# A q/kv group turned token-major: 512 + 192 columns, ScalarE sums of squares, and latents turned back by transposes

## The chip, the cores and the metric

The kernel runs on one core of one Trainium2 chip. The metric is the device time of one execution in microseconds (us). TensorE multiplies matrices: it loads a stationary operand of up to 128 x 128 and streams the columns of a moving operand past it. VectorE, ScalarE and GpSimd do the elementwise work, SyncE issues most of the DMAs.

## The reference

Two layers of a streaming encoder over 256 positions of width 2048. The part that the change touches is the latent attention's input: of the projection `h @ w_in`, 704 columns are the query latent (384), the key/value latent (256) and a rotary key (64).

```
proj = h @ w_in[l]
uv, q_c, kv_c, k_r, sb, sc, sh, ag = jnp.split(proj, IN_SPLITS, axis=-1)
def rms_norm(x, gain, eps=RMS_EPS):
    y = xf * lax.rsqrt(jnp.mean(jnp.square(xf), axis=-1, keepdims=True) + eps)
    return y * gain
...
q = rms_norm(q_c, q_norm_g) @ w_uq            # 4 heads of 128 + 64 (rotary)
kv = rms_norm(kv_c, kv_norm_g) @ w_ukv        # 4 heads of 128 + 128
k_rope = apply_rope(k_r, cos, sin)
... scores, block-causal mask, softmax, times v
```

Beside this stand a gated MLP (columns u, v), a short convolution (sb, sc, sh), and a convolution of 31 taps (ag), then an output projection and a feed-forward block. All of it is float32.

## The kernel before

The projection is computed in groups of columns, in the order D (the ag columns), U and V, B (the q/kv columns), C (sc and sh), E (sb). A group runs over 16 k-tiles of 128 rows of `w_in`, two or four of them a unit. `run` calls `stream` for each unit: it loads the unit's weights (`weights`), issues the products of the unit before, advances the modulation stream (`pump`: a DMA of `w_mod` and a `macc` step on VectorE, L235), and takes `bg` pieces of background work. When a group's last products have been issued, its `then` function follows: for group B that is `mix_b`, the whole attention, followed in program text by group C's products.

In the first layer group B's weights are plain float32 tiles (`wexact`), multiplied by the normalised input `hF`. In the second layer each weight tile is split in two parts of type fp32r: ScalarE makes `whi` (L455), VectorE makes `wlo` (L456), and three products are taken, whi with hT's high and low part, wlo with the high part.

Group B before is channel-major: a 128 x 128 block of weights is stationary, 256 tokens stream past, and six blocks of 128 channels (768 columns, the last 64 of them unused) fill three PSUM banks of 2 x 256. `mix_b` then squares five blocks on ScalarE (`sqB`), sums the squares over partitions with ten matmuls against ones (`ps_ss`), makes rr on VectorE, raises it to -0.5 on GpSimd (`power`, L105), spreads the kv part over partitions by a diagonal matrix and a matmul (`dgB`, `ps_rkv`), and multiplies kvr by it. The q norm is applied later, in the softmax scale. `qg`, `kvr` and `kc` feed the matmuls `ps_qn`, `ps_kn`, `ps_v` and `ps_kr`.

Background work in both layers is, above all, the 31-tap convolution of group D: `tap(j, k)` is one instruction on VectorE over 128 channels (convD, L834; in the changed file L868), 120 of them a layer. In the text they are queued a few per unit (`STEPS`: B takes 7 a unit in the first layer, 5 in the second). The instructions' final order on each engine is not that of the text: a scheduler in the framework lists them by readiness when the program is built, and each engine's list is then fixed.

PSUM has six banks for group sums (`accp`) and two for the rest (`msp`); weight splits have four buffers each of whi and wlo.

Of the kernel before, what the change touches and what calls it, by code (L numbers as in the profile page):

```python
# [39 lines left out]
STEPS = [  # L40
    dict(B=7, C=8, up=2),
    dict(U=6, B=5, C=6, E=6, up=2),
]
# [7 lines left out]
def encoder_kernel(ctx: ExitStack, tc: tile.TileContext, A: dict, consts: bass.AP, out: bass.AP):  # L51
    nc = tc.nc
    pe, act, dve, pool = nc.tensor, nc.scalar, nc.vector, nc.gpsimd
# [7 lines left out]
    smallp = ctx.enter_context(tc.tile_pool(name="smallp", bufs=2))  # L61
# [7 lines left out]
    def tmp_tile(name):  # L69
        return tmpp.tile([P, 512], F32, tag="tmp", name=name)  # L70

    def ms_tile(name):
        return msp.tile([P, 512], F32, tag="ms", name=name)

    def acc_tile(name):
        return accp.tile([P, 512], F32, tag="acc", name=name)

    def mm(o, lhsT, rhs, start, stop):
        pe.matmul(o, lhsT, rhs, start=start, stop=stop, skip_group_check=True)  # L79
# [4 lines left out]
    def slot(name, dtype=F32):  # L84
        return slotp.tile([P, 1024], dtype, tag="slot", name=name)
# [4 lines left out]
    ident = cst[:, 0:128]  # L90
# [3 lines left out]
    cosT = cst[:, 512:768]  # L94
    sinT = cst[:, 768:1024]
# [3 lines left out]
    ones = ones_r.bitcast(F32)  # L99
# [367 lines left out]
    hT = []  # L467
# [9 lines left out]
    def group(w, c0, width, name, then, ntm=0, nk=2, hF=None, bg=0, spare=0):  # L477

        ncm = (width - 512 * ntm) // P
        box = {}

        def products(item, u):
            if u == 0:
                box["c"] = [acc_tile(f"{name}_c{i}") for i in range((ncm + 1) // 2)]
                box["t"] = [[acc_tile(f"{name}_t{t}{i}") for i in range(ntm)] for t in range(2)]
                box["h"] = list(hT)
            for part in (range(0, min(4, ncm)), range(4, ncm)):
                for k, (hi, lo) in enumerate(item):  # L490
# [36 lines left out]

    def group2(w, c0, name, then, bg=0, spare=0):
# [21 lines left out]

        return KT // nk, load, products, lambda: then(box["c"]), bg

    hN, first = [], []

    def first_group(w, c0, then):
# [251 lines left out]
    def mixers(l, w_in, Y, hF=None, between=None):  # L807
        pm = PM[l]
        CW = lambda k, j: pm[:, k * 4 + j : k * 4 + j + 1]
        QG = lambda j: pm[:, 124 + j : 125 + j]  # L810
        KVG = lambda j: pm[:, 127 + j : 128 + j]
# [135 lines left out]
                )  # L947


        def mix_b(cps, _):  # L950
# [9 lines left out]
            qg = slot("qg")[:, :768].rearrange("p (j s) -> p j s", j=3)  # L960
            kvr = slot("kvr")[:, :768].rearrange("p (j s) -> p j s", j=3)
            bank = [(cps[i // 2], (i % 2) * S) for i in range(6)]
            sq = [tmp_tile("sqB0"), tmp_tile("sqB1"), tmp_tile("sqB2")]
            sqs = []
            for i in range(5):
                ps, o = bank[i]
                s = sq[i // 2][:, (i % 2) * S : (i % 2) * S + S]
                act.activation(out=s, in_=ps[:, o : o + S], func=AF.Square)
                sqs.append(s)
            for j in range(3):  # L970
                ps, o = bank[j]
                act.activation(out=qg[:, j, :], in_=ps[:, o : o + S], func=AF.Copy, scale=QG(j))
            for j in range(2):
                ps, o = bank[3 + j]
                dve.tensor_scalar(out=kvr[:, j, :], in0=ps[:, o : o + S], scalar1=KVG(j), scalar2=None, op0=ALU.mult)
            ps, o = bank[5]
            kc, ks = tmp_tile("kc"), None
            dve.tensor_tensor(out=kc[0:64, 0:S], in0=ps[0:64, o : o + S], in1=cosT[0:64, :], op=ALU.mult)
            dve.tensor_tensor(out=kc[0:64, S : 2 * S], in0=ps[0:64, o : o + S], in1=sinT[0:64, :], op=ALU.mult)
            ps = ms_tile("ps_ss")  # L980
# [6 lines left out]
            dve.tensor_scalar(  # L987
                out=rr[:, 0:2], in0=ps[:, 0:2], scalar1=1.0 / Q_LORA, scalar2=RMS_EPS, op0=ALU.mult, op1=ALU.add
            )
            dve.tensor_scalar(  # L990
                out=rr[:, 2:4], in0=ps[:, 2:4], scalar1=1.0 / KV_LORA, scalar2=RMS_EPS, op0=ALU.mult, op1=ALU.add
            )
            power(rr[:, 4:8], rr[:, 0:4])
            dve.tensor_scalar(out=rr[:, 4:6], in0=rr[:, 4:6], scalar1=ATT_SCALE, scalar2=None, op0=ALU.mult)
            dg = tmp_tile("dgB")
            for t in range(2):
                dve.tensor_scalar(
                    out=dg[:, t * P : (t + 1) * P], in0=ident, scalar1=rr[:, 6 + t : 7 + t], scalar2=None, op0=ALU.mult
                )
            ps = ms_tile("ps_rkv")  # L1000
            mm(ps[:, :S], ones, dg[:, :S], True, True)
            for j in range(2):
                dve.tensor_tensor(out=kvr[:, j, :], in0=kvr[:, j, :], in1=ps[:, :S], op=ALU.mult)

            rope = slot("rope").rearrange("p (j s) -> p j s", j=4)
            ps = ms_tile("ps_kr")
# [167 lines left out]
    def by_pieces(l, w_in, hF, between, mix_d, mix_u, gelu_v, mix_v, mix_b, mix_c, mix_e):  # L1174
# [50 lines left out]
        for q, (k0, nkt) in enumerate(PIECES):  # L1225
# [42 lines left out]
            gelu_v(t, sums["V"][t])  # L1268
        mix_v()
        phase(l, "B")  # L1270
        run(group(w_in, C_Q, 768, f"B{l}", mix_b, hF=hf, bg=STEPS[l]["B"]))
        phase(l, "C")

        def mix_ce(cps, tps):
# [260 lines left out]
```

## Time and profile before

| | us |
|---|---|
| median of three runs | 2290.1 |
| lowest and highest | 2289.65, 2292.27 |
| profiled execution | 2285.5 |
| its span | 2283.7 |

In the profile's rows PE is TensorE's matmuls and PEld its weight loads, DVE is VectorE, ACT is ScalarE, POOL is GpSimd, SPq the queue from which SyncE issues DMAs. A row of the timeline gives the start and the length in us of a merged run of equal instructions, its line, what it writes and reads, and how many there are (xN); in brackets, how long the engine had idled before it and what ended that. Matmuls overlap, so what one costs in a stream is read from the distance of two starts, not from its length. A plain float32 matmul shows as two records, an fp32r one as one. A row of the waits gives total us, times, longest. L79 is the helper that issues nearly all matmuls, so its rows are told apart by tile names.

### The profile page before, as it was taken

What the parts mean: (1) busy time and instruction counts of PE and PEld (TensorE: products, weight loads), DVE (VectorE), ACT (ScalarE), POOL (GpSimd) and SP (SyncE); (2) the same over time, 40 slices, a digit from 0 to 9 for tenths busy, and PEclk for the clock granted to TensorE, in tenths of its full rate; (3) what the DMA queues carried; (4) which work ended last, traced back from release to release, by engine and by line L of the source; (5) the groups of instructions that cost most, each with busy time, mean ns of one, the idle gap of its engine ahead of it and who ended that gap; (6) DMA issues with size and microseconds to landing.
All of it is one profiled execution on the core that took longest, in us unless ns stands there. A gap on an engine that the chain in (4) does not pass through costs nothing. (4 is left out here: it accounts for less than half of the span.)

```text
span 2283.7 us, 30024 instructions
## 1 busy us (share of the span) xinstructions
PE 2226.7 (98%) x11682; PEld 1859.8 (81%) x11682; DVE 1788.8 (78%) x2270; ACT 1049.8 (46%) x1525; POOL 35.3 (2%) x59
## 2 busy tenths in 40 slices
PE   5899999999999999999999999999999999999998
PEld 4688886478888888887887999877888888888886
DVE  6878998598888898998976799787776565665676
ACT  2221141355554544544556434556555554454553
POOL 2000000000000000000000000000000000000000
PEclk9999999999999999999999999999999999999999
DMA  9999889778998988888974666876765556555554
GB/s 348 368 335 342 304 301 393 301 267 304 319 329 302 323 312 327 317 316 304 319 258 148 200 214 240 291 268 223 247 223 190 184 182 199 186 196 190 193 194 147
DMA packets 224566, 605.21 MB, mean 265 GB/s; under 512 B 14548, under 2 KB 27076, under 8 KB 202660
## 3 DMA queue, kind: packets, MB, share of 16 engines
q1 hardware_dynamic: 223576, 602.30, 74.7%
q8 instruction: 91, 1.49, 0.3%
q0 software_dynamic: 848, 1.01, 0.1%
q14 instruction: 51, 0.42, 0.0%
HBM read 601.16 MB, written 2.10 MB: 264 GB/s over the span
## 5 line engine op out<-in xcount | busy, mean ns | idle before, releaser
L456 DVE TENSOR_TENSOR wlo<-wraw,whi 128x1024 fp32r<-128x1024 f32 (+1 forms) x624 | 749.6, 1214 | 315.5 <-ACT whi L455 309.4
L455 ACT CAST whi<-wraw 128x1024 fp32r<-128x1024 f32 (+1 forms) x624 | 649.2, 1047 | 727.2 <-PE g_c L79 204.4
L79 PE MATMUL v_c<-hT,whi 128*128 128x512 f32 x1408 | 493.1, 394 | 0.0
L79 PE MATMUL g_c<-hT,whi 128*128 128x512 f32 x1280 | 448.2, 394 | 0.0
L79 PE MATMUL v_c<-hT,wlo 128*128 128x256 f32 x1408 | 394.3, 280 | 0.0
L79 PE MATMUL d<-whi,a 128*128 128x512 f32 x1344 | 387.9, 390 | 0.0
L235 DVE SCALAR_TENSOR_TENSOR macc<-wmod,cact,macc 128x2048 f32<-128x2048 f32 x150 | 351.6, 2344 | 17.1 <-DMA wmod<-in_w_mod_dram 16.8
L79 PE MATMUL g_c<-hT,wlo 128*128 128x256 f32 x1280 | 358.4, 280 | 0.0
L79 PEld LDWEIGHTS v_c<-hT,whi 128*128 128x128 f32 x1408 | 263.9, 187 | 61.0
L79 PEld LDWEIGHTS d<-whi,a 128*128 128x128 f32 x1344 | 252.9, 188 | 52.4
L79 PEld LDWEIGHTS g_c<-hT,whi 128*128 128x128 f32 x1280 | 239.9, 187 | 55.6
L79 PEld LDWEIGHTS v_c<-hT,wlo 128*128 128x128 f32 x1408 | 265.8, 189 | 0.2
L79 PEld LDWEIGHTS g_c<-hT,wlo 128*128 128x128 f32 x1280 | 241.7, 189 | 0.2
L79 PE MATMUL d<-wlo,a 128*128 128x512 f32 x672 | 233.8, 390 | 1.9 <-DVE wlo L456 1.9
L79 PEld LDWEIGHTS d<-wlo,a 128*128 128x128 f32 x672 | 126.6, 188 | 29.1 <-DVE wlo L456 2.7
L79 PE MATMUL o<-whi,a 128*128 128x512 f32 x352 | 102.3, 398 | 2.3 <-ACT whi L455 2.3
L834 DVE SCALAR_TENSOR_TENSOR convD<-gluD,pm,convD 128x237 f32<-128x237 f32 (+26 forms) x240 | 99.0, 458 | 0.5
L474 ACT CAST a<-g 128x512 fp32r<-128x512 f32 x132 | 81.1, 616 | 36.7 <-PE d L79 34.2
L79 PE MATMUL D_c<-hT,whi 128*128 128x256 f32 x448 | 85.7, 292 | 4.0 <-ACT hT L474 3.0
L475 DVE TENSOR_TENSOR a<-g,a 128x512 fp32r<-128x512 f32 x132 | 87.5, 683 | 1.8 <-ACT a L474 1.8
L566 PE MATMUL first<-wexact,hN 128*128 128x512 f32 x192 | 85.7, 596 | 1.5 <-ACT hN L82 1.2
L235 DVE SCALAR_TENSOR_TENSOR qacc<-wmod,cact,qacc 128x1024 f32<-128x1024 f32 (+1 forms) x75 | 80.2, 1070 | 2.4 <-DMA wmod<-in_w_mod_dram 0.4
(311 smaller groups left out, 2462.3 us busy)
## 6 DMA issues: line engine op xcount, KB each, us to landing
wraw<-in_ffn_w_up_dram SPq DMA_DIRECT2D x168, 1024.0 KB, 5.2
wmod<-in_w_mod_dram SPq DMA_DIRECT2D x160, 1024.0 KB, 6.6
wraw<-in_ffn_w_down_dram SPq DMA_DIRECT2D x88, 1024.0 KB, 5.3
wmod<-in_w_mod_dram SPq DMA_DIRECT2D x64, 512.0 KB, 7.9
wraw<-in_w_in_dram SPq DMA_DIRECT2D x30, 1024.0 KB, 5.5
wexact<-in_w_in_dram SPq DMA_DIRECT2D x52, 512.0 KB, 6.7
wraw<-in_w_out_dram SPq DMA_DIRECT2D x24, 1024.0 KB, 7.3
wexact<-in_w_out_dram SPq DMA_DIRECT2D x16, 512.0 KB, 11.0
```

The costliest lines, as they stand in the source:

```text
L79: pe.matmul(o, lhsT, rhs, start=start, stop=stop, skip_group_check=True)
L235: i = dve.scalar_tensor_tensor(out=acc, in0=w, scalar=col, in1=acc, op0=ALU.mult, op1=ALU.add)
L455: held(act.copy(hi[:, :m], r), "cast")
L456: i = dve.tensor_tensor(out=lo[:, :m], in0=r, in1=hi[:, :m].bitcast(F32), op=ALU.subtract)
L474: act.copy(hi, src)
L475: dve.tensor_tensor(out=lo, in0=src, in1=hi.bitcast(F32), op=ALU.subtract)
L566: i = pe.matmul(ps, hN[kt // 4][:, kt % 4, t * P : (t + 1) * P], parts[kt], start=kt == 0, stop=kt == KT - 1, skip_group_check=True,)
L834: dve.scalar_tensor_tensor(out=yd[:, j, 30 - k :], in0=glu[:, j, : S - 30 + k], scalar=CW(k, j), in1=yd[:, j, 30 - k :], op0=ALU.mult, op1 ...
```

## The change

Group B becomes token-major in both layers (`latent_group`): 128 tokens are stationary, and 512 + 192 weight columns stream past, for two token tiles. The sums are `B_w` (two banks, 512 columns each) and `B_n` (one bank, 192 columns for each tile). The 64 unused columns are no longer loaded or multiplied. Since a token is now a partition, ScalarE accumulates each token's sum of squares while squaring (`accum_out`), straight into `ss`; the ten matmuls of `ps_ss`, the diagonal and `ps_rkv` go. ScalarE copies the q columns and the rotary key out of PSUM, and, after GpSimd's power, the kv columns scaled by rr. Twelve transposes on TensorE (L1025, tiles `ps_q` and `ps_kv`) bring the latents back to channel-major, from where ScalarE makes `qg` and VectorE `kc` and `kvr`.

```
-            bank = [(cps[i // 2], (i % 2) * S) for i in range(6)]
-            for i in range(5):
-                act.activation(out=s, in_=ps[:, o : o + S], func=AF.Square)
-            for j in range(3):
-                act.activation(out=qg[:, j, :], in_=ps[:, o : o + S], func=AF.Copy, scale=QG(j))
-            for j in range(2):
-                dve.tensor_scalar(out=kvr[:, j, :], in0=ps[:, o : o + S], scalar1=KVG(j), ...)
...
-                for j in range(3):
-                    mm(ps[:, t : t + 1], sqs[j][:, t * P : (t + 1) * P], ones[:, 0:1], j == 0, j == 2)
-                for j in range(2):
-                    mm(ps[:, 2 + t : 3 + t], sqs[3 + j][:, t * P : (t + 1) * P], ones[:, 0:1], j == 0, j == 1)
...
-            mm(ps[:, :S], ones, dg[:, :S], True, True)
-            for j in range(2):
-                dve.tensor_tensor(out=kvr[:, j, :], in0=kvr[:, j, :], in1=ps[:, :S], op=ALU.mult)
+    def latent_group(w, c0, name, then, hF=None, bg=0):
+        nk = 2
...
+            for k, (hi, lo) in enumerate(item):
+                for t in range(2):
+                    tok = slice(t * P, (t + 1) * P)
+                    outs = ((box["wide"][t], slice(0, 512), st), (box["narrow"][t], slice(512, 704), st and t == 0))
+                    if lo is None:
+                        for o, c, first in outs:
+                            mm(o, hF(kt)[:, tok], hi[:, c], first, sp)
+                        continue
+                    xh, xl = (h[:, kt % 2, tok] for h in box["h"][kt // 2][:2])
+                    for o, c, first in outs:
+                        mm(o, xh, hi[:, c], first, False)
+                    for o, c, _ in outs:
+                        mm(o, xh, lo[:, c], False, False)
+                    for o, c, _ in outs:
+                        mm(o, xl, hi[:, c], False, sp)
...
+            for t in range(2):
+                pieces = ((0, lat[t][:, 0:384], wide[t][:, 0:384], Q_LORA),)
+                pieces += ((2, lat[t][:, 384:512], wide[t][:, 384:512], KV_LORA), (4, rest[t][:, 0:128], narrow[t][:, 0:128], KV_LORA))
+                for at, junk, ps, n in pieces:
+                    act.activation(out=junk, in_=ps, func=AF.Square, scale=float(n) ** -0.5, accum_out=ss[:, at + t : at + t + 1])
+                act.copy(lat[t][:, 0:384], wide[t][:, 0:384])
+                act.copy(rest[t][:, 128:192], narrow[t][:, 128:192])
...
+            power(rr[:, 4:8], rr[:, 0:4])
+            for t in range(2):
+                for o, ps in ((lat[t][:, 384:512], wide[t][:, 384:512]), (rest[t][:, 0:128], narrow[t][:, 0:128])):
+                    act.activation(out=o, in_=ps, func=AF.Copy, scale=rr[:, 6 + t : 7 + t])
+            def turn(ps, o, parts):
+                for t in range(2):
+                    pe.transpose(ps[0:n, o + t * P : o + (t + 1) * P], parts[t], ident)
+                return ps[:, o : o + S]
...
-        run(group(w_in, C_Q, 768, f"B{l}", mix_b, bg=STEPS[l]["B"]))
+        run(latent_group(w_in, C_Q, f"B{l}", mix_b, bg=STEPS[l]["B"]))
```

The order on the engines moves too. VectorE in the middle of the second layer's group B, before; wlo is a weight split (one for each k-tile), convD a tap, macc a step of the modulation:

```order
L456 TENSOR_TENSOR wlo<-wraw,whi 128x768
L834 SCALAR_TENSOR_TENSOR convD<-gluD,pm_104,convD 128x227
L456 TENSOR_TENSOR wlo<-wraw,whi 128x768
L834 SCALAR_TENSOR_TENSOR convD<-gluD,pm_104,convD 128x226
L235 SCALAR_TENSOR_TENSOR macc<-wmod,cact,macc 128x2048
L834 SCALAR_TENSOR_TENSOR convD<-gluD,pm_104,convD 128x248
L456 TENSOR_TENSOR wlo<-wraw,whi 128x768
L834 SCALAR_TENSOR_TENSOR convD<-gluD,pm_104,convD 128x247
L456 TENSOR_TENSOR wlo<-wraw,whi 128x768
```

The same place in the changed kernel, from the eighth split to the ninth:

```order
L456 TENSOR_TENSOR wlo<-wraw,whi 128x704
L868 SCALAR_TENSOR_TENSOR convD<-gluD,pm_104,convD 128x246
L868 SCALAR_TENSOR_TENSOR convD<-gluD,pm_104,convD 128x254
L868 SCALAR_TENSOR_TENSOR convD<-gluD,pm_104,convD 128x245
L868 SCALAR_TENSOR_TENSOR convD<-gluD,pm_104,convD 128x253
L868 SCALAR_TENSOR_TENSOR convD<-gluD,pm_104,convD 128x244
L868 SCALAR_TENSOR_TENSOR convD<-gluD,pm_104,convD 128x252
L868 SCALAR_TENSOR_TENSOR convD<-gluD,pm_104,convD 128x243
L456 TENSOR_TENSOR wlo<-wraw,whi 128x704
```

Between most of the later splits six or seven taps now stand where one to seven stood; they come from behind group B. From the fourth split to the first rr VectorE has 45 taps and one macc before, 91 taps, two macc and two splits of ya (`a`) after.

VectorE where group B of the second layer ends, before (kvr and kc read the group's sums, rr the sums of squares):

```order
L975 TENSOR_SCALAR kvr<-B_c_10109,pm_104 128x256
L834 SCALAR_TENSOR_TENSOR convD<-gluD,pm_104,convD 128x227
L975 TENSOR_SCALAR kvr<-B_c_10110,pm_104 128x256
L834 SCALAR_TENSOR_TENSOR convD<-gluD,pm_104,convD 128x226
L978 TENSOR_TENSOR kc<-B_c_10110,cst 64x256
L979 TENSOR_TENSOR kc<-B_c_10110,cst 64x256
L987 TENSOR_SCALAR rr<-ps_ss 128x2
L990 TENSOR_SCALAR rr<-ps_ss 128x2
```

and in the changed kernel, where rr comes first and eleven taps and a macc stand between the last split and it:

```order
L868 SCALAR_TENSOR_TENSOR convD<-gluD,pm_104,convD 128x231
L868 SCALAR_TENSOR_TENSOR convD<-gluD,pm_104,convD 128x230
L235 SCALAR_TENSOR_TENSOR macc<-wmod,cact,macc 128x2048
L1008 TENSOR_SCALAR rr<-ss 128x2
L1009 SCALAR_TENSOR_TENSOR rr<-ss 128x2
L868 SCALAR_TENSOR_TENSOR convD<-gluD,pm_104,convD 128x229
L1013 TENSOR_SCALAR rr<-rr 128x2
L1037 TENSOR_TENSOR kc<-ps_q,cst 64x256
```

rr moved ahead of kc and kvr, which now need the transposes.

TensorE in the changed kernel, second layer, around the kv transposes, with group C's matmuls between them (lat holds the latents of a token tile):

```order
L79 MATMUL C_c_10619<-hT,whi 128x256 x2
L79 MATMUL C_c_10619<-hT,wlo 128x256
L1025 MATMUL ps_kv<-cst,lat_10396 128x128
L79 MATMUL C_c_10620<-hT,whi 128x256 x2
L79 MATMUL C_c_10620<-hT,wlo 128x256
L1025 MATMUL ps_kv<-cst,lat_10397 128x128
L79 MATMUL C_c_10620<-hT,whi 128x256
L79 MATMUL ps_kr<-kc,cst 128x256 x2
L1025 MATMUL ps_kv<-cst,lat_10398 128x128 x2
```

where before one matmul spread the kv scale:

```order
L79 MATMUL C_c_10734<-hT,whi 128x256
L79 MATMUL ps_rkv<-dgB,ones 128x256
L79 MATMUL ps_kr<-kc,cst 128x256 x2
L79 MATMUL C_c_10734<-hT,whi 128x256
L79 MATMUL C_c_10734<-hT,wlo 128x256
```

24 matmuls of group C stand ahead of the first kv transpose and 33 ahead of ps_qn; before, 44 stood ahead of ps_qn.

More of the change, by code (lines that the diff above doesn't have):

```diff
@@ L551, in group2, with products, load @@
         return KT // nk, load, products, lambda: then(box["c"]), bg
+    def latent_group(w, c0, name, then, hF=None, bg=0):
+        nk = 2
+        box = {}
+        def products(item, u):
+            if u == 0:
+                box["wide"] = [acc_tile(f"{name}_w{t}") for t in range(2)]
+                both = acc_tile(f"{name}_n")
+                box["narrow"] = [both[:, t * 192 : (t + 1) * 192] for t in range(2)]
+                box["h"] = list(hT)
+            for k, (hi, lo) in enumerate(item):
+                kt = u * nk + k
+                st, sp = kt == 0, kt == KT - 1
+                for t in range(2):
[12 more added lines that the diff above has]
+                        mm(o, xl, hi[:, c], False, sp)
+        def load(u):
+            return weights(w, u * nk, nk, c0, 704, hF is not None)
+        return KT // nk, load, products, lambda: then(box["wide"], box["narrow"]), bg
     hN, first = [], []
@@ L947, in mix_v, with mix_b @@
                 )
-        def mix_b(cps, _):
+        def mix_b(wide, narrow):
             wq0, wq1, wkv = raw_tile("wq0"), raw_tile("wq1"), raw_tile("wkv")
@@ L987, in mix_b @@
[L987 to L991, printed above, removed]
+            lat = [tmp_tile("lat0"), tmp_tile("lat1"), tmp_tile("lat2")]
+            rest = [lat[2][:, t * 192 : (t + 1) * 192] for t in range(2)]
+            ss = smallp.tile([P, 8], F32, tag="rr", name="ss")
@@ L992, in mix_b @@
+            rr = smallp.tile([P, 8], F32, tag="rr", name="rr")
+            dve.tensor_scalar(out=rr[:, 0:2], in0=ss[:, 0:2], scalar1=RMS_EPS, scalar2=None, op0=ALU.add)
+            dve.scalar_tensor_tensor(
+                out=rr[:, 2:4], in0=ss[:, 2:4], scalar=RMS_EPS, in1=ss[:, 4:6], op0=ALU.add, op1=ALU.add
             )
@@ L994, in mix_b @@
             dve.tensor_scalar(out=rr[:, 4:6], in0=rr[:, 4:6], scalar1=ATT_SCALE, scalar2=None, op0=ALU.mult)
[L995 removed]
             for t in range(2):
[L997 to L1000, printed above, removed]
[L1001 to L1003 removed]
+                for o, ps in ((lat[t][:, 384:512], wide[t][:, 384:512]), (rest[t][:, 0:128], narrow[t][:, 0:128])):
+                    act.activation(out=o, in_=ps, func=AF.Copy, scale=rr[:, 6 + t : 7 + t])
+            qg = slot("qg")[:, :768].rearrange("p (j s) -> p j s", j=3)
+            kvr = slot("kvr")[:, :768].rearrange("p (j s) -> p j s", j=3)
+            def turn(ps, o, parts):
+                for t in range(2):
+                    n = parts[t].shape[1]
+                    pe.transpose(ps[0:n, o + t * P : o + (t + 1) * P], parts[t], ident)
+                return ps[:, o : o + S]
+            ps = ms_tile("ps_q")
+            for j in range(2):
+                by = turn(ps, j * S, [lat[t][:, j * P : (j + 1) * P] for t in range(2)])
+                act.activation(out=qg[:, j, :], in_=by, func=AF.Copy, scale=QG(j))
+            ps = ms_tile("ps_q")
+            by = turn(ps, 0, [lat[t][:, 256:384] for t in range(2)])
+            act.activation(out=qg[:, 2, :], in_=by, func=AF.Copy, scale=QG(2))
+            by = turn(ps, S, [rest[t][:, 128:192] for t in range(2)])
+            kc = tmp_tile("kc")
+            dve.tensor_tensor(out=kc[0:64, 0:S], in0=by[0:64, :], in1=cosT[0:64, :], op=ALU.mult)
+            dve.tensor_tensor(out=kc[0:64, S : 2 * S], in0=by[0:64, :], in1=sinT[0:64, :], op=ALU.mult)
+            ps = ms_tile("ps_kv")
+            for j in range(2):
+                by = turn(ps, j * S, [lat[t][:, 384:512] if j == 0 else rest[t][:, 0:128] for t in range(2)])
+                dve.tensor_scalar(out=kvr[:, j, :], in0=by, scalar1=KVG(j), scalar2=None, op0=ALU.mult)
             rope = slot("rope").rearrange("p (j s) -> p j s", j=4)
@@ L1270, in by_pieces @@
         phase(l, "B")
-        run(group(w_in, C_Q, 768, f"B{l}", mix_b, hF=hf, bg=STEPS[l]["B"]))
+        run(latent_group(w_in, C_Q, f"B{l}", mix_b, hF=hf, bg=STEPS[l]["B"]))
         phase(l, "C")
```

18 lines of the change are left out of this document (3 added, 15 removed).

## The prediction

> **What bounds the kernel now.** I read the busy shares first, then TensorE's own waits, then busy time by stage around the two places where the q/kv group (group B) runs, then the rows of the timeline there.
>
> The first row is from the page's busy shares; then come TensorE's waits from 1299 to 1441 us; then three stages (length; busy us and instructions of TensorE, its weight loads, VectorE, ScalarE, GpSimd; clock; DMA share; GB/s): group B of the second layer, the attention behind it, group B of the first layer.
>
> ```profile
> PE 2226.7 (98%) x11682; PEld 1859.8 (81%) x11682; DVE 1788.8 (78%) x2270; ACT 1049.8 (46%) x1525; POOL 35.3 (2%) x59
> ...
> PE ps_mix L79 <- POOL wT L915: 1.8, 1, 1.8
> PE ps_rD L79 <- DVE dgD L874: 0.3, 1, 0.3
> ...
> 1299.30:1337.70 38.40, 36.59 (x307) 36.38 (x305) 38.23 (x73) 15.62 (x25) 0.86 (x3) 1.00 0.68 214
> 1337.70:1385.00 47.30, 47.15 (x316) 42.42 (x315) 44.84 (x94) 18.33 (x34) 1.12 (x1) 1.00 0.66 232
> ...
> 190.00:233.00 43.00, 43.00 (x208) 37.87 (x208) 41.55 (x81) 9.02 (x19) 2.83 (x5) 1.00 0.92 324
> ```
>
> TensorE carries the time: a microsecond taken from it or made to wait on it counts in full. In the second layer VectorE is just as full (38.23 of 38.40 us in group B, 44.84 of 47.30 behind it), yet TensorE waits there for only 2.1 us in 142. The two engines are balanced to about a microsecond, by the order in which VectorE's work stands: whatever is put ahead of a weight split on VectorE, TensorE will wait for. In the first layer group B has no splits (plain fp32 weights) and TensorE is busy without a gap, with the DMA at 0.92.
>
> **Products.** Group B alone on TensorE, second layer and first; then rows that price one matmul, from their starts.
>
> ```profile
> 1299.30:1337.90 38.60, 34.94 (x288) 34.67 (x288) 0.00 (x0) 2.04 (x7) 1.00 0.68 213
> 189.80:233.10 43.30, 41.59 (x192) 36.25 (x192) 0.00 (x0) 2.15 (x7) 1.00 0.92 325
> ...
> 1699.87 0.39 PE L79 MATMUL v_c<-hT,whi 128*128 128x512 f32 x1
> 1700.10 0.28 PE L79 MATMUL v_c<-hT,wlo 128*128 128x256 f32 x1
> 1700.22 0.39 PE L79 MATMUL v_c<-hT,whi 128*128 128x512 f32 x1
> ...
> 263.67 9.66 PE L79 MATMUL C_c<-hF,wexact 128*128 128x256 f32 x44
> ...
> 257.51 3.60 PE L79 MATMUL ps_v<-wkv,kvr 128*128 128x512 f32 x8
> ```
>
> First layer: a plain fp32 matmul is two records; 256 columns take 2 x 9.66/44 = 0.44 us (0.43 without the last one's tail), 512 columns 2 x (3.60 - 0.59)/7 = 0.86. They scale with columns, so 192 take 0.32. Before, 96 x 0.43 = 41.3 us; after, 32 x (0.86 + 0.32) = 37.8. TensorE has 3.5 us less.
>
> Second layer (fp32r splits): 256 columns take 34.94/288 = 0.12 us, 512 take 0.23 (1699.87 to 1700.10). 192 columns stand in no row. Lower bound 0.09 (in proportion to 256), upper 0.32 (the plain rate above, the nearest row that is slower). I take 0.12, the nearest row of the same type, and keep both ends. Before 288 x 0.12 = 34.6; after 96 x (0.23 + 0.12) = 33.6: 1.0 less, with the ends -3.8 and +18.2.
>
> [...]
>
> The weight tiles lose 64 of 768 columns, so DMA has less to bring: no cost.
>
> **mix_b on TensorE.** Rows of the matmuls taken out, of transposes like those put in, of accumulating ScalarE instructions, and of the power on GpSimd.
>
> ```profile
> 233.28 0.95 PE L79 MATMUL ps_ss<-ones,sqB 128*128 128x1 f32 x8
> 234.61 1.40 PE L79 MATMUL ps_ss<-ones,sqB 128*128 128x1 f32 x12
> 240.27 0.59 PE L79 MATMUL ps_rkv<-dgB,ones 128*128 128x256 f32 x2
> 281.45 0.60 PE L1101 MATMUL ps_pT<-cst,p 128*128 128x128 f32 x4
> ...
> 270.59 0.46 ACT L1082 ACTIVATE p<-ps_sc,sm,rr 128x128 f32<-128x128 f32 x1
> 271.04 0.45 ACT L1082 ACTIVATE p<-ps_sc,sm,rr 128x128 f32<-128x128 f32 x1
> ...
> 236.41 2.99 POOL L105 TENSOR_TENSOR rr<-rr,mhalf 128x4 f32<-128x4 f32 x1 [32.40 <-DVE rr L990]
> ```
>
> Out: 0.95 + 1.40 + 0.43 = 2.8 us a layer. In: 12 transposes at (0.60 - 0.27)/3 = 0.11, 1.3 us. TensorE has 1.5 us less a layer.
>
> In return it waits on a longer chain. The latents must be squared and copied by ScalarE before a transpose: an accumulating instruction of 128 columns comes every 0.45 us, so three squares and two copies a token tile are 1.9 to 2.4 us by these rows, the first tile's partly under the second's products. The kv columns wait further: VectorE's rr, GpSimd's power (1.12 us below, 2.99 here, where a macc ran beside it), a scaling copy. In the first layer I count 1.7 us of new waits up to there (0.2 and 0.4 for the two copies, twice 0.6 at the kv transposes; bounds 0 and 4, if the power takes 2.99), with group C's matmuls between them as cover. Further on stands the attention:
>
> ```profile
> 273.03 0.86 DVE L1092 TENSOR_SCALAR p<-p,sm 128x128 f32<-128x128 f32 x4
> 273.44 0.83 PE L1101 MATMUL ps_pT<-cst,p 128*128 128x128 f32 x4
> ```
>
> The transposes of p started while VectorE was just finishing p: no slack. VectorE's work up to there gets no shorter, so some 1.5 us of the gain becomes a wait there. First layer: -3.5 - 1.5 + 1.7 + 1.5 = **-1.8 us**, bounds -5.0 (no wait) and +2.
>
> **VectorE's order, second layer.** This decides. The order of VectorE's instructions, in the section on the change, has between group B's fourth weight split and the first rr: before, 45 conv taps (convD) and 1 macc; after, 91 taps and 2 macc, and two splits of ya. The trace of before shows VectorE running its rows in the order printed, without a gap:
>
> ```profile
> 1322.03 0.95 DVE L456 TENSOR_TENSOR wlo<-wraw,whi 128x768 fp32r<-128x768 f32 x1
> 1322.90 2.79 DVE L834 SCALAR_TENSOR_TENSOR convD<-gluD,pm,convD 128x244 f32<-128x244 f32 x7
> 1325.62 0.95 DVE L456 TENSOR_TENSOR wlo<-wraw,whi 128x768 fp32r<-128x768 f32 x1
> ...
> 1340.45 0.41 DVE L978 TENSOR_TENSOR kc<-B_c,cst 64x256 f32<-64x256 f32 x1
> 1340.79 0.40 DVE L979 TENSOR_TENSOR kc<-B_c,cst 64x256 f32<-64x256 f32 x1
> 1341.12 0.14 DVE L987 TENSOR_SCALAR rr<-ps_ss 128x2 f32<-128x2 f32 x1
> 1341.47 1.12 POOL L105 TENSOR_TENSOR rr<-rr,mhalf 128x4 f32<-128x4 f32 x1 [37.49 <-DVE rr L990]
> 1342.62 0.17 DVE L994 TENSOR_SCALAR rr<-rr 128x2 f32<-128x2 f32 x1 [0.91 <-POOL rr L105]
> 1343.09 2.35 DVE L235 SCALAR_TENSOR_TENSOR macc<-wmod,cact,macc 128x2048 f32<-128x2048 f32 x1
> 1345.35 0.74 DVE L1003 TENSOR_TENSOR kvr<-kvr,ps_rkv 128x256 f32<-128x256 f32 x2
> ...
> L475 DVE TENSOR_TENSOR a<-g,a 128x512 fp32r<-128x512 f32 x132 | 87.5, 683 | 1.8 <-ACT a L474 1.8
> ...
> 1346.99 5.42 PE L79 MATMUL ps_qn<-qg,wq 128*128 128x256 f32 x24
> ```
>
> By starts a tap takes (1325.62 - 1322.90)/7 = 0.39 us, a macc 2.26, a ya split at most 0.68, a weight split of 768 columns 0.87 (0.07 less for 704). So rr moves by 46 x 0.39 + 2.26 + 2 x 0.62 - 13 x 0.07 - 1.5 (two kvr and two kc, now behind rr) = +19.0: from 1341.1 to 1360.1. The last split of group B, by the same count, starts near 1345 instead of 1331, so TensorE, at 0.35 us a pair, ends the group near 1347.6 (before: 1337.8) after some 10 us of waits on wlo. Then it turns the q columns and does 24 of group C's matmuls, 3.8 us in all, and stands before the kv transposes until rr (1360.1), the power (1.5 us from rr to its product) and one scaling copy (0.5) are through: 1362.1, a wait of about 10. Another 2.4 us of work (4 transposes, 9 of C, two of ps_kr) and 0.8 of waits bring ps_qn to 1365.3, against 1346.99; and 11 matmuls of C fewer lie behind it (33 against 44 by the order), 1.3 us. Second layer: **+19.6 us**. Bounds: +12 if a third of the moved work falls where VectorE would have idled, +24 if narrow products cost the upper end and the waits behind them stay. What VectorE has done early it need not do later, but TensorE's waits there are 0.3 us: nothing is paid back.
>
> **Sum.** -1.8 + 19.6 = +17.8. The profiled execution took 2285.5 us (span 2283.7) and the median of the runs is 2290.1, 4.6 above it; I add to the median: **2307.9 us**.
>
> **Rivals.** (1) Narrow fp32r matmuls cost what plain fp32 does, 0.32 us. Nothing in the trace shows fp32r under 256 columns, so nothing excludes it. TensorE then needs 96 x 0.55 = 52.8 us and ends the group near 1356 without waiting for splits; the chain through rr still ends at 1362: 2308 to 2311. [...] (2) Half of the lag is paid back, since VectorE has fewer taps left behind rr: 2290.1 - 1.8 + 9.8 = 2298. Against it stand the 0.3 us. (3) The other side: faster. TensorE never meets the moved taps, and the products' and mix_b's savings arrive: -3.5 - 1.0 - 3.0 + 1.7 = -5.8, 2284.3. That needs the lag on VectorE under about 6 us, a tap at 0.1 us where the row has 0.39, or splits that were ready that much ahead; the balance of 38.23 in 38.40 speaks against it.
>
> **How the numbers follow.** Forecast 0.53, rival (1) 0.33, rival (2) 0.07, rival (3) 0.05; 0.02 for others. A change under 0.2% (4.6 us) can't be told from none here. Forecast and (1) are slower; of (2) a part ends within 0.2%. So slower 0.90, same 0.05, faster 0.05. Range: low 2290.1 - 5.0 + 12 = 2297, high 2290.1 + 2 + 24 = 2316, drawn in to 2314 as both ends together are unlikely; it leaves out (3) and little else.
>
> **What would show it.** In the profile after: rr of the second layer about 19 us behind its old place relative to the start of group B; TensorE waiting on wlo for some 10 us and at ps_kv for about as long (forecast), or B_n's narrow matmuls 0.32 us apart, group B some 56 us long and no wait on wlo (rival 1). Group B of the first layer 39.8 us long instead of 43.3. I am wrong if VectorE reaches rr within 6 us of its old place, or if TensorE behind the attention has caught up.

## The result, and the profile after

| | before | after |
|---|---|---|
| median of six runs, us | 2290.7 | 2309.1 |
| lowest to highest | 2287.1 to 2296.6 | 2303.7 to 2310.5 |
| profiled execution (span) | 2285.5 (2283.7) | 2310.3 (2308.5) |

The changed kernel is slower by a ratio of 1.0075, with a 95% interval of [1.0058, 1.0091]: 17.2 us [13.3, 20.8]. The ratio is an estimate over all runs; the two medians are 18.4 us apart. The two profiled executions are 24.8 us apart: each is one execution, and the six runs of one kernel spread over 7 to 10 us. So places and mechanisms are read below from the profiles, and totals from the timed runs.

The busy shares of the changed kernel, from its page:

```profile
PE 2226.5 (96%) x11502; PEld 1842.2 (80%) x11502; DVE 1787.2 (77%) x2262; ACT 1055.1 (46%) x1555; POOL 33.7 (1%) x59
```

TensorE's four longest waits from 1300 to 1470 us (total us, times, longest):

```profile
PE B_w L79 <- DVE wlo L456: 7.7, 7, 1.2
PE ps_kv L1025 <- ACT lat L1016: 7.5, 1, 7.5
PE C_c L79 <- DVE wlo L456: 2.8, 2, 1.6
PE ps_mix L79 <- POOL wT L949: 2.1, 1, 2.1
```

Group B of the second layer and the attention behind it, busy time by stretch (columns as in the prediction's stages):

```profile
1300.40:1348.70 48.30, 38.51 (x211) 32.04 (x209) 48.03 (x106) 14.61 (x23) 0.31 (x1) 0.96 0.47 142
1348.70:1400.00 51.30, 40.81 (x226) 34.83 (x225) 32.98 (x55) 17.92 (x42) 1.71 (x3) 0.87 0.57 201
```

TensorE is busy for as long as before (2226.5 us against 2226.7) in a longer span, so in that count the loss is all waiting. But work at half clock counts as busy too (4.00 of 4.00 us at a clock of 0.50 in the row from 1366 us, below). From group B's first product to the start of group E's last one, before and then after:

```profile
1299.34:1440.59 141.25, 139.02 (x1059) 133.01 (x1058) 129.87 (x230) 62.19 (x95) 3.05 (x5) 1.00 0.66 227
1300.44:1465.36 164.92, 144.19 (x952) 130.49 (x951) 129.25 (x225) 65.17 (x110) 3.02 (x5) 0.95 0.56 192
```

Of the 23.7 us lost there, 18.5 are waiting (20.7 us instead of 2.2), and 5.2 are longer work, though there is less to do; half clock, below, accounts for 4.2 of it. Group B lasts 48.3 us instead of 38.6, all of it full on VectorE (48.03), with 106 of its instructions there instead of 74. Behind it VectorE, 44.84 us busy in 47.30 before, is busy for only 32.98 in 51.30: it had done that work early, and TensorE got nothing back for it.

The timeline at the place that decides, with VectorE's rr, GpSimd's power, and TensorE's kv transposes:

```profile
1359.59 2.35 DVE L235 SCALAR_TENSOR_TENSOR macc<-wmod,cact,macc 128x2048 f32<-128x2048 f32 x1
1361.85 0.16 DVE L1008 TENSOR_SCALAR rr<-ss 128x2 f32<-128x2 f32 x1
1362.22 1.10 POOL L105 TENSOR_TENSOR rr<-rr,mhalf 128x4 f32<-128x4 f32 x1 [58.27 <-DVE rr L1009]
1363.77 0.48 PE L1025 MATMUL ps_kv<-cst,lat 128*128 128x128 f32 x1 [7.51 <-ACT lat L1016]
1365.25 2.07 PE L79 MATMUL ps_kr<-kc,cst 64*128 64x256 f32 x4
1368.80 3.53 PE L79 MATMUL ps_qn<-qg,wq 128*128 128x256 f32 x8
```

TensorE stood for 7.5 us, since rr was late. What the prediction did not have is in the granted clock (the last but two column) of the same stretch:

```profile
1354.00:1358.00 4.00, 1.89 (x14) 1.69 (x14) 3.75 (x9) 0.47 (x1) 0.00 (x0) 1.00 0.65 223
1358.00:1362.00 4.00, 0.00 (x0) 0.00 (x0) 3.89 (x8) 0.00 (x0) 0.00 (x0) 0.56 0.09 39
1362.00:1366.00 4.00, 2.23 (x8) 1.91 (x9) 2.48 (x9) 1.14 (x4) 1.71 (x3) 0.50 0.73 228
1366.00:1370.00 4.00, 4.00 (x14) 3.06 (x13) 1.74 (x3) 2.61 (x4) 0.00 (x0) 0.50 0.09 36
1370.00:1374.00 4.00, 4.00 (x15) 3.28 (x14) 1.56 (x2) 0.70 (x2) 0.00 (x0) 0.74 0.36 66
1374.00:1378.00 4.00, 4.00 (x24) 3.59 (x23) 0.75 (x2) 1.23 (x2) 0.00 (x0) 1.00 0.49 201
```

While TensorE stood, the clock fell to half, and it stayed there until 1372.1: of the 8.3 us after TensorE had gone on, half (4.2 us) was lost, an estimate from the granted 0.50. The 24 records of ps_qn show the pace: eight took 3.30 us up to 1372.1, at 0.50, and sixteen the 3.53 us behind it, at 1.00.

### The profile page after: what moved, and what is told of

Same layout as the page of the kernel before. It is cut to its first block, busy times and chain, and to the rows that moved or that the text cites. A ratio compares the mean times of both kernels' runs of the same rounds, so it can differ in the third digit from the quotient of the medians.

```text
span 2308.5 us, 29683 instructions
## 1 busy us (share of the span) xinstructions
PE 2226.5 (96%) x11502; PEld 1842.2 (80%) x11502; DVE 1787.2 (77%) x2262; ACT 1055.1 (46%) x1555; POOL 33.7 (1%) x59
## 5 line engine op out<-in xcount | busy, mean ns | idle before, releaser
L868 DVE SCALAR_TENSOR_TENSOR convD<-gluD,pm,convD 128x237 f32<-128x237 f32 (+24 forms) x240 | 98.8, 458 | 0.6
```

Source lines behind the costliest of these rows:

```text
L868: dve.scalar_tensor_tensor(out=yd[:, j, 30 - k :], in0=glu[:, j, : S - 30 + k], scalar=CW(k, j), in1=yd[:, j, 30 - k :], op0=ALU.mult, op1 ...
```

## The experiments

Theory A: the loss lies in the second layer, in the order in which VectorE's work was listed when the program was built (conv taps ahead of weight splits and of rr); the half clock is its sequel; the token-major form itself gains a little. Theory B: the longer chain (ScalarE's sums, rr, power, scaled copies, transposes) costs, whatever the order. Theory C: a narrow fp32r product is dear on the chip.

In the table, "taps" counts the conv taps that VectorE's list has between the fourth weight split of the second layer's group B and the first rr; rr is its last part's start after the group's first product; "B to E" runs from that product to the start of group E's last one; the wait is the longest of TensorE inside it; "half" is the time at half clock inside it. All of that is from one profiled execution each; the ratio to the kernel before, with its 95% interval, is from the timed runs, each kernel against runs of the kernel before in the same session.

| kernel | taps | rr, us | wait, us | half, us | B to E, us | ratio |
|---|---|---|---|---|---|---|
| before | 45 | 42 | 1.8 | 0 | 141.3 | 1 |
| after (512 + 192) | 91 | 61 | 7.5 | 17.1 | 164.9 | 1.0075 [1.0058, 1.0091] |
| 448 + 256 | 35 | 36 | 1.0 | 0 | 137.5 | 0.9972 [0.9960, 0.9984] |
| 450 + 254 | 95 | 67 | 6.7 | 27.3 | 173.0 | 1.0103 [1.0077, 1.0128] |
| taps held | 45 | 46 | 5.0 | 6.8 | 150.0 | 1.0020 [1.0008, 1.0031] |
| taps and step held | 45 | 40 | 2.1 | 10.2 | 145.1 | 0.9998 [0.9986, 1.0011] |
| first layer only | 45 | 42 | 1.6 | 3.4 | 142.3 | 0.9984 [0.9971, 0.9997] |
| second layer only | 91 | 61 | 7.5 | 17.1 | 164.9 | 1.0093 [1.0075, 1.0111] |
| before, 12 taps a unit | 88 | 60 | 5.6 | 13.7 | 160.4 | 1.0076 [1.0055, 1.0096] |
| wait filled, 14 | 91 | 61 | 3.7 | 10.2 | 167.2 | 1.0123 [1.0102, 1.0145] |
| wait filled, 8 | 91 | 61 | 4.2 | 3.4 | 164.0 | 1.0089 [1.0075, 1.0103] |

From the start of E's last product to the start of the last product of all (d), ten of these profiles have 831.6 to 832.6 us and one 834.1; nothing that was lost before is given back there.

### 448 + 256 columns

```
-   box["narrow"] = [both[:, t * 192 : (t + 1) * 192] for t in range(2)]
-   outs = ((box["wide"][t], slice(0, 512), st), (box["narrow"][t], slice(512, 704), st and t == 0))
+   box["narrow"] = [both[:, t * 256 : (t + 1) * 256] for t in range(2)]
+   outs = ((box["wide"][t][:, 0:448], slice(0, 448), st), (box["narrow"][t], slice(448, 704), st and t == 0))
    ... and mix_b reads its pieces from there
```

> The changed kernel with the 704 columns cut into 448 + 256 instead of 512 + 192, in both layers; nothing else is changed, and no step of the chain behind the sums is shorter. VectorE's order as built comes back with it: between the fourth weight split of the second layer's B and the first rr stand 35 conformer taps (91 in the changed kernel, 45 in the kernel before). Theory A (VectorE's order in the second layer is the cost, and TensorE's half clock after the wait is its sequel; the token-major form itself gains a little): rr of the second layer at about 1342 instead of 1361.9, no wait over 3 us at ps_kv, no stretch at clock 0.50 behind it, and 2284 to 2291 us. Theory B (the longer chain from the last product through ScalarE's sums, rr, the power and the transposes costs by itself): the wait at ps_kv stays at 5 us or more, and 2297 us or more. Theory C (a product of 192 columns is dear, one of 256 is not): the last B product comes earlier by 5 us or more while VectorE's waits stay, about 2303.

Measured: 2280.3 us against 2288.0, by the ratio 6.4 us faster than the kernel before [3.7, 9.2], and below theory A's 2284 to 2291. All of TensorE's waits from 1300 to 1470 us (the one at ps_mix, 1.0 us, had ended before):

```profile
PE ps_kv L1025 <- ACT qg L1031: 0.8, 1, 0.8
PE ps_qn L79 <- ACT rope L1051: 0.5, 1, 0.5
PE ps_rD L79 <- DVE dgD L908: 0.3, 1, 0.3
```

The two parts of rr in both layers (lengths in ns, then the first and the last start):

```profile
L1008 DVE TENSOR_SCALAR rr<-ss x2: 169/169/169, 230.7 to 1330.2; 128x2 f32<-128x2 f32 x2
L1009 DVE SCALAR_TENSOR_TENSOR rr<-ss x2: 153/157/161, 231.6 to 1331.8; 128x2 f32<-128x2 f32 x2
```

The second layer's rr (the later of the two starts in each row) comes at 1331.8, earlier than the expected 1342, and neither the long wait nor the half clock is there. The chain behind rr is as long as in the changed kernel, so it is not what cost (B). Nothing else was taken away, so VectorE's order, its sequels and TensorE's own pace are what is left.

### Two columns moved: 450 + 254

```
-   outs = ((box["wide"][t][:, 0:448], slice(0, 448), st), (box["narrow"][t], slice(448, 704), st and t == 0))
+   outs = ((box["wide"][t][:, 0:450], slice(0, 450), st), (box["narrow"][t][:, 0:254], slice(450, 704), st and t == 0))
    ... and mix_b reads its pieces from there
```

> The kernel with 448 + 256 columns, with two columns moved from the narrow half to the wide one: 450 + 254, in both layers. All else is the same, the number of products, of columns and of instructions on each engine too. As built, VectorE has 95 taps between the fourth weight split of the second layer's B and the first rr (35 with 448 + 256, 91 with 512 + 192): the order flips between a narrow product of 256 columns and one of 254. Theory A, with the build-time scheduler's price for a product under 256 columns as the origin of the order: TensorE's own pace is that of 448 + 256 (a pair in about 0.32 us), rr comes at 1360 or later, a wait of 6 us or more at ps_kv or splits that come late, and the time is that of the changed kernel or above, 2304 to 2314 us. If the chip itself is slower below 256 columns: pairs of 0.4 us and more. If neither: 2278 to 2285 us, as with 448 + 256.

Measured: 2314.1 us, 1.0103 [1.0077, 1.0128], the slowest but one, at the upper edge of theory A's 2304 to 2314. TensorE's pace in the second layer's group B, from the timeline of the 448 + 256 kernel:

```profile
1316.29 0.36 PE L79 MATMUL B_w<-wlo,hT 128*128 128x448 f32 x1
1316.49 0.28 PE L79 MATMUL B_n<-wlo,hT 128*128 128x256 f32 x1
1316.61 0.36 PE L79 MATMUL B_w<-whi,hT 128*128 128x448 f32 x1
```

The same of the 450 + 254 kernel:

```profile
1329.75 0.37 PE L79 MATMUL B_w<-whi,hT 128*128 128x450 f32 x1
1329.95 0.28 PE L79 MATMUL B_n<-whi,hT 128*128 128x254 f32 x1
1330.07 0.37 PE L79 MATMUL B_w<-wlo,hT 128*128 128x450 f32 x1
```

And what TensorE waited for there, from 1290 to 1470 us:

```profile
PE B_w L79 <- DVE wlo L456: 13.1, 9, 2.0
PE ps_kv L1025 <- ACT lat L1016: 6.7, 1, 6.7
PE C_c L79 <- DVE wlo L456: 3.8, 2, 2.1
```

A pair takes 0.32 us in both (1316.29 to 1316.61, 1329.75 to 1330.07), and 254 columns the same 0.12 as 256. TensorE's products are not slower, and the work is nearly the same; what differs is the order, by 60 taps, and with it some 30 us. A step of the modulation sums stands straight ahead of rr as well, and it had to wait for its weights:

```profile
1361.37 2.35 DVE L235 SCALAR_TENSOR_TENSOR macc<-wmod,cact,macc 128x2048 f32<-128x2048 f32 x1 [4.37 <-DMA wmod<-in_w_mod_dram]
```

So of the 67 us until rr, the taps are not all. That the scheduler prices a product under 256 columns higher, and so thinks TensorE slow enough for VectorE to take taps first, is an estimate from the two lists (35 taps with 256 columns, 95 with 254); no run here shows its price.

### Taps held behind their splits

```
+   last_split[0] = i.ins.name                      # in weights(), at each wlo
+   if l == 1:                                       # in tap()
+       tc.add_manual_dep(i.ins, last_split[0], order_dep, ...)
```

> The changed kernel, 512 + 192 columns as it is, with one constraint of order added in the second layer: a conformer tap may not be listed ahead of its unit's last weight split. On VectorE 45 taps now stand between the fourth weight split of the second layer's B and the first rr, instead of 91. Theory A: as with 45 taps before, rr at about 1342 to 1346, the wait at ps_kv under 4 us, 2284 to 2293 us. Theory B: rr is early and the time is not, 2297 us or more, since the chain behind rr sets it. Theory C: 2300 us or more, since the 192 columns stay.

Measured: 2291.8 us, 1.0020 [1.0008, 1.0031]. With 512 + 192 columns as they are, three quarters of the loss are gone. The time is in theory A's span, but the wait at ps_kv, 5.0 us, is more than the 4 that A allowed. The timeline names it:

```profile
1340.84 2.35 DVE L235 SCALAR_TENSOR_TENSOR macc<-wmod,cact,macc 128x2048 f32<-128x2048 f32 x1 [1.85 <-DMA wmod<-in_w_mod_dram]
1343.11 0.16 DVE L1012 TENSOR_SCALAR rr<-ss 128x2 f32<-128x2 f32 x1
1344.95 0.48 PE L1029 MATMUL ps_kv<-cst,lat 128*128 128x128 f32 x1 [5.02 <-ACT lat L1020]
```

One step of the modulation sums stands straight ahead of rr, had to wait for its own weights, and holds rr for 4.2 us (1.85 of waiting, 2.35 of work).

### That step held as well

```
+   msteps.append(i)                                 # in mod_step(), at each macc
+   if l == 1:                                       # in mix_b, after the second kvr
+       for step in msteps[-1:]:
+           tc.add_manual_dep(step.ins, i.ins.name, order_dep, ...)
```

> The kernel with the taps held (512 + 192 columns, 45 taps ahead of rr), with one more constraint: the step of the modulation sums (macc, 2.35 us, which waited 1.85 us for its weights) that stood on VectorE straight ahead of rr goes behind the second kvr. What is left of the loss there was a wait of 5.0 us at ps_kv and 6.8 us at half clock. Theory A (TensorE waits for whatever VectorE has ahead of rr, and the clock follows): the wait at ps_kv falls to 1 us or less, no half clock in this place, 2282 to 2288 us. Theory B (the longer chain of the token-major form): the wait keeps at least 3 us, since the power and the scaled copies stay, 2289 to 2293 us.

As built, neither of the two steps that stood between the fourth split and rr stands there any more. Measured: 2288.0 us, 0.9998 [0.9986, 1.0011]: at the edge of what A expected. The loss is gone and the wait at ps_kv too; yet half clock came again, 10.2 us of it, which A had excluded. The timeline of ScalarE and TensorE there:

```profile
1337.13 0.37 ACT L1023 ACTIVATE lat<-B_w,rr 128x128 f32<-128x128 f32 x1 [2.35 <-POOL rr L105]
1338.14 0.49 ACT L1038 ACTIVATE qg<-ps_q,pm 128x256 f32<-128x256 f32 x1
1338.69 0.44 PE L1032 MATMUL ps_q<-cst,lat 128*128 128x128 f32 x2 [2.09 <-ACT qg L1038]
```

ScalarE's list now has the four scaled copies, which wait for rr, ahead of the qg copies, for which TensorE's PSUM tile waits. So theory B has a small part: the chain through rr can hold ScalarE as it can hold VectorE, here for 2.1 us and what the clock adds.

### One layer at a time

```
first layer only:   the second layer runs group() and the old mix_b
second layer only:  the first layer runs group() and the old mix_b
```

> The first layer in the changed form (token-major, 512 + 192), the second layer in the form of the kernel before (channels on partitions, 768 columns). Theory A: the loss is all in the second layer, so this is the kernel before with the first layer's own gain: 2286 to 2291 us, B of the first layer 3.5 us shorter as in the changed kernel, rr of the second layer no later than before by over 2 us. Theory B: each layer loses some by its longer chain; the first layer alone then gives 2293 us or more. A third thing to read: the changed kernel lost 2 us between 497 and 605 us, in the feed-forward of the first layer; if the first layer's form does that, it is here too.

> The other half: the second layer in the changed form (token-major, 512 + 192 columns), the first in the form of the kernel before. On VectorE 91 taps stand ahead of the second layer's rr, as in the changed kernel. Theory A: the whole loss is here, and the first layer's gain is missing: 20 to 25 us above the kernel before, 2308 to 2313 us. If both layers lose: 2300 us or less.

Measured: the first layer alone gains 3.7 us [0.7, 6.6] (2285.9); the second alone loses 21.3 us [17.2, 25.4] (2310.2). Both were expected so (the first at the lower edge of its 2286 to 2291), and they add up: -0.16% and +0.93% make +0.77%, where both together measured +0.75%. One expectation missed: in the profile of the first kernel, its slowest of twelve executions, the first layer's group B was not 3.5 us shorter. It lasted 43.7 us (43.5 before), with a wait that the changed kernel's profile does not have, and 3.4 us at half clock behind it:

```profile
205.19 0.71 PE L79 MATMUL ps_mix<-wT,va 128*128 128x128 f32 x4 [1.90 <-DVE va L957]
```

So the first layer's gain rests on the timed runs; its interval begins close to nothing. The 2 us that the changed kernel's profile lost between 497 and 605 us can't be told from scatter: from the end of the first layer's group C to the start of the second layer's group B, the eleven profiles have 966.6 to 977.4 us, and the two lowest are one kernel with the old first layer and one with the new.

### The old form with the new order

```
-    dict(U=6, B=5, C=6, E=6, up=2),
+    dict(U=6, B=12, C=6, E=6, up=2),       # in the kernel before
```

> The kernel before with one number changed: 12 conformer taps are written into each unit of the second layer's B instead of 5. The form of the sums, the columns and the chain behind rr are the old ones; but on VectorE 88 taps instead of 45 now stand between the fourth weight split and rr (91 in the changed kernel). Theory A: the order alone costs, whatever the form: rr at 1355 to 1362 instead of 1341.1, TensorE waits for weight splits in B and behind it, 2298 to 2310 us. Theory B (the new form's chain is what costs): within 4 us of the kernel before.

Measured: 2304.7 us, 1.0076 [1.0055, 1.0096]. One number in the kernel before, and it loses as much as the change does. rr came at 1352.1, 60 us after the group's start, a little earlier than expected on the clock and 18 us later than before relative to that start. Here it is late splits that TensorE waits for, by its waits from 1292 to 1455 us:

```profile
PE B_c L79 <- DVE wlo L456: 11.8, 3, 5.6
```

### The wait filled

```
     ps = ms_tile("ps_kv")
+    if l == 1:
+        for _ in range(14):                          # 8 in the second kernel
+            mm(ps[:, :S], ident, cosT, True, True)
```

> The changed kernel with 14 products of constants (128x128 by 128x256, plain fp32, some 0.43 us each, 6.0 us together) put into TensorE's 7.5 us wait ahead of the transposes of ps_kv in the second layer; their result is written over and read by nobody. VectorE's order is that of the changed kernel word for word, so rr stays at about 1361.9. Theory A with the clock as a cost of its own: the wait no longer lowers the granted clock, so the 24 ps_qn products take about 5.4 us instead of 7.0 and the ps_kr pair 1.1 instead of 2.1; the stretch from ps_kv to the end of E is 3 to 4.5 us shorter, about 2305 us. If the low clock has another cause than the idle stretch: the same 0.50 behind it, and 2308 to 2310 us.

> The changed kernel with 8 products of constants (3.4 us together, the same as the 14 before) in the wait at ps_kv of the second layer. With 14 of them the order behind kvr had moved, and a new wait of 3.7 us stood there; with 8 both kvr stay ahead of the weight splits. About 4 us of the wait stay empty. If it is the empty stretch that lowers the clock, and one of 4 us is too short for 13.7 us of it: 0 to 6.8 us at half clock instead of 13.7, ps_kr back to 1.1 us or in part, 2 to 4 us faster than the changed kernel, 2304 to 2308 us. If the low clock has another cause: 13.7 us of it again and 2308 to 2311 us.

With 14, neither of the expected times came: 1.0123 [1.0102, 1.0145], slower than the changed kernel. The filled part was as expected (the ps_kr pair took 1.13 us instead of 2.07, at full clock). But the expectation said that VectorE's order was the same, and it was so only up to rr: behind it a weight split had moved ahead of the first kvr, and the split had to wait for a transfer, as the timeline shows.

```profile
1366.88 1.99 ACT L455 CAST whi<-wraw 128x1024 fp32r<-128x1024 f32 x2 [2.55 <-DMA wraw<-in_w_in_dram]
1367.96 1.23 DVE L456 TENSOR_TENSOR wlo<-wraw,whi 128x1024 fp32r<-128x1024 f32 x1 [2.60 <-ACT whi L455]
1369.10 0.48 DVE L1045 TENSOR_SCALAR kvr<-ps_kv,pm 128x256 f32<-128x256 f32 x1
1369.63 0.69 PE L1025 MATMUL ps_kv<-cst,lat 128*128 128x128 f32 x2 [3.72 <-DVE kvr L1045]
```

A new wait of 3.7 us, and half clock again, from 1365.6 to 1372.4; it began 0.3 us before that wait did, and 2.0 us after the filled one had ended. With 8 fillers both kvr stand ahead of the splits. The timeline of TensorE:

```profile
1360.18 0.33 PE L1025 MATMUL ps_kv<-cst,lat 128*128 128x128 f32 x1 [4.17 <-ACT lat L1016]
1364.37 5.55 PE L79 MATMUL ps_qn<-qg,wq 128*128 128x256 f32 x24
```

The clock by stretch in the same kernel:

```profile
1361.00:1365.00 4.00, 4.00 (x15) 3.12 (x15) 2.08 (x5) 1.37 (x3) 0.00 (x0) 0.57 0.45 183
1365.00:1369.00 4.00, 4.00 (x20) 3.53 (x19) 2.14 (x2) 1.94 (x3) 0.00 (x0) 1.00 0.23 20
```

Half clock lasted 3.4 us instead of 13.7, and the 24 ps_qn products took 5.4 us (1364.37 to the next group at 1369.75) where the changed kernel takes 6.8 (1368.80 to 1375.63). So in these two profiles less standing goes with less half clock; one profile of each does not make it a rule, and the last section has kernels that don't fit one. The time, 2307.0 us, lies in the expected 2304 to 2308, but the gain of 2 to 4 us over the changed kernel can't be seen: 1.0089 [1.0075, 1.0103] against 1.0075, overlapping, and 1 us in B to E. By the granted 0.50 the half clock costs 1.7 us there (half of the 3.4) instead of 4.2, an estimate, so 2.5 are saved. The fillers had taken the place of six group C products (27 ahead of ps_qn instead of 33 in the list), 0.7 us, and a new wait of 0.8 us stands at ps_qr, for VectorE's qc; what is left is smaller than the scatter.

## Why the prediction was right

**VectorE's order** was right in mechanism and in most numbers. rr was to come 19.0 us later; relative to the group's start it came 19.6 later (61.4 against 41.8 us). Group B was to end 48.3 us after its start; it ended after 48.4. TensorE was to wait some 10 us on wlo in group B (7.7, and 2.8 more on group C's), and some 10 at ps_kv (7.5). The old form with 12 taps a unit, the two columns moved and the held taps show that the order is the cause, and not only goes with it.

**The second layer's total** was too small in the profiles: +19.6 predicted, +23.7 there; timed it is 21.3 [17.2, 25.4], an interval that holds both. Of the 4.1 us between, 0.5 came ahead of the first kv transpose (63.3 us after the group's start, 62.8 by the prediction). The step that was mis-sized is "Another 2.4 us of work", which with 0.8 of waits was to bring ps_qn to 1365.3, by the old rows' speed: it took 5.0 us (1363.77 to 1368.80) instead of 3.2, because TensorE worked at half clock (0.50 all through). So ps_qn came 68.4 us after the group's start, not 66.0. It then ran on at half clock to 1372.1, which lost 1.7 us more (half of 3.3, by the same estimate). (The 11 matmuls of group C that the prediction calls fewer behind ps_qn are 11 more, 33 instead of 44 standing ahead of it; it adds their 1.3 us, as it must.)

Half clock came with the long wait: the wait began at 1356.3, the clock fell at 1358.5, 2.2 us later, and it came back at 1372.1, after 8.3 us of work. The prediction, which forecast a wait of 10 us, had no such stretch in it. The profile of before has two waits of about 2 us, each with 3.4 us at half clock close behind it. The timeline of TensorE there:

```profile
372.85 1.19 PE L79 MATMUL o<-whi,a 128*128 128x512 f32 x4 [2.27 <-ACT whi L455]
1080.00 0.50 PE L79 MATMUL d<-wlo,a 128*128 128x512 f32 x1 [1.91 <-DVE wlo L456]
```

The clock by stretch in the same profile:

```profile
374.12:377.52 3.40, 3.40 (x8) 2.73 (x9) 3.33 (x2) 0.00 (x0) 0.00 (x0) 0.50 1.01 424
1080.68:1084.08 3.40, 3.40 (x10) 2.65 (x9) 3.40 (x4) 0.00 (x0) 0.00 (x0) 0.50 1.04 397
```

The wait of 1.8 us at ps_mix has none behind it (1.00 in the prediction's row of group B). So by the rows of before alone a stretch at half clock behind a wait of 10 us was likely, not certain, and its length could not be read from them.

**The first layer** came out better than forecast in this profile: -1.8 predicted, -3.4 from the group's start to the end of group C (135.4 to 132.0 us). Timed alone it gained 3.7 us [0.7, 6.6], which holds 1.8 as well. The stretch of group B in the changed kernel, with TensorE busy throughout:

```profile
191.00:231.00 40.00, 40.00 (x149) 24.55 (x148) 38.65 (x74) 8.38 (x18) 2.22 (x3) 1.00 0.93 319
```

All of TensorE's waits from 190 to 325 us there:

```profile
PE ps_kv L1025 <- ACT qg L1031: 1.2, 1, 1.2
```

The products' term held (39.8 us predicted; 39.7 from the first product, 191.04, to the first transpose, 230.71). The term that failed is "some 1.5 us of the gain becomes a wait there", at ps_pT: there is no such wait. The new waits at ps_kv were counted as 1.7 and are 1.2. How large the error is stays open: the eight profiles with the new first layer have 132.0 to 136.4 us from group B's start to group C's end, 133.6 in the mean, the three with the old one 135.4 to 137.5, 136.1 in the mean. None of the eight has a wait at ps_pT, but four have one of 1.2 to 2.2 us at ps_mix in group B, which none of the three has and the prediction did not count. The row behind the failed term showed that transposes started while VectorE was still finishing p; that was a start without slack, not a wait.

In the two profiles the errors, -1.6 and +4.1 us, have opposite signs and partly cancel. The sum was +17.8; timed, it is 17.2 [13.3, 20.8]. That it came within 0.6 us is luck in part; that the second layer's order decides is not.

**Products in the second layer**: the price of 192 columns was taken as 0.12, with 0.09 as the lower end. The rows:

```profile
1347.29 0.41 PE L79 MATMUL B_w<-whi,hT 128*128 128x512 f32 x1
1347.54 0.25 PE L79 MATMUL B_n<-whi,hT 128*128 128x192 f32 x1
1347.63 0.41 PE L79 MATMUL B_w<-whi,hT 128*128 128x512 f32 x1
```

The narrow one takes 0.09 us and a pair 0.34, against 0.35 predicted. The wide one takes 0.25 where 0.23 was taken, and 448 columns take 0.20 beside a narrow 256: so 512 + 192 costs 0.34 a pair and 448 + 256 costs 0.32, for the same 704 columns, 2 us in group B.

**The rivals.** (1), narrow products at the plain rate with group B 56 us long, fell by these rows; it had been given 0.33, too much for a rate that only lay next to an unknown. (2), half of the lag paid back: refuted, since every profile has the same length behind group E. (3), faster: refuted for this kernel, but it is what the 448 + 256 kernel does. Its condition was that rr comes less than 6 us late; there it came 5.5 us early (36.3 against 41.8), and the time is 6.4 us less, where the rival had 5.8.

## What to carry to other kernels

When two engines are balanced to a microsecond, compare the lists of instructions that the build made on both before any price: here two columns moved from one product to another, at no cost in TensorE's own pace (0.32 us a pair in both), turned a gain of 6 us into a loss of 24. Where an in-order engine feeds the bound one, look at what stands straight ahead of the instruction that the bound engine waits for (a tap, a step that waits for a transfer, a copy that waits for a later result), and hold that back. Price a wait of several microseconds on TensorE together with the half clock that can come with it: single profiles here had 3.4, 6.8 and 13.7 us of it with waits of 4.2, 5.0 and 7.5 us at ps_kv.

## What the hardware showed beside that

In six profiles (before, after, 450 + 254, first layer only, second layer only, and before with 12 taps a unit) half clock came in steps of about 3.4 us, but for the stretch that runs past the program's end: single stretches measured 3.40 to 3.42, 6.82 to 6.84, 10.24 and 13.66 us. Their lengths do not follow the waits ahead of them. In the kernel with taps and step held, TensorE stood for only 2.1 us, the clock fell all the same, and it stayed at half for 10.2 us although TensorE was busy through all of them; after 5.0 us of standing (taps held) it was 6.8 us, after 4.2 (wait filled, 8) 3.4. The wait at ps_mix early in the second layer's group B, 1.7 to 2.2 us in most kernels, came with 3.4 us at half in three of the eleven profiles (with waits of 1.7, 2.0 and 2.1), and with none in others (1.8, 1.9, 2.0 and 2.2). And with the first layer alone changed, 3.4 us at half began at about 1343.1 while TensorE was busy without a gap. What makes the clock fall, and for how long, was not settled here.
